# Layer 0's memory keys and values ahead of the mixer, whose input is normed before its projections

## The chip, the core and the metric

The kernel runs on one core of a Trainium2 chip. Its time is the device time of one execution in microseconds (us). The engines of the core that matter are TensorE (PE in the profile, PEld for its weight loads), VectorE (DVE), ScalarE (ACT), GpSimd (POOL) and SyncE (SP), which here only issues DMA transfers.

## The reference

The reference is a two-layer decoder trunk on one sequence of 512 tokens with 1024 channels, with 256 memory tokens beside it. All of it is float32. Cut to what the change touches:

```python
def mixer_ab(x, norm, w_in, ...):
    z = rms_norm(x, norm) @ w_in                 # 1024 -> 2560
    z_gate, z_rec, z_pool = z[..., :1024], z[..., 1024:2048], z[..., 2048:]
    xr = causal_dwconv(z_rec, conv_w, conv_b)    # 4 taps
    y_a = jax.nn.gelu(z_gate) * rg_lru(xr, ...)  # two gates, then a linear recurrence
    y_b = multi_scale_pool(z_pool, ...)          # trailing means of 2, 4, 8, 16 tokens
    return jnp.concatenate([y_a, y_b], axis=-1) @ w_out

def cross_attn(x, mem, norm, mem_norm, wq, wk, wv, wo):
    q = rms_norm(x, norm) @ wq
    m = rms_norm(mem, mem_norm)
    k, v = m @ wk, m @ wv
    ...                                          # 4 heads, softmax, then @ wo
```

Each layer is a token mixer (in layer 0 `mixer_ab`, in layer 1 a Conformer convolution), then `cross_attn`, then a gated MLP with a short convolution, each added to `x`. A last RMS norm follows. `mem` is the same in both layers; the gains and the weights are not.

## The kernel before

**Layout.** Channels lie on the 128 partitions and tokens along the free dimension, so `x` is eight tiles of 128 x 512. A weight is loaded in pieces of 128 x 1024 (512 KB). A float32 product is made of three passes of a faster format over exact parts: each operand is split into a high part (ScalarE, line 147) and a low part (VectorE or GpSimd, line 148), and `mm3` (lines 151 to 155) issues high x high, high x low and low x high. A projection of one 128-channel column chunk (`project`, line 207) is thus 24 matmuls of 512 columns; one key piece is 24 matmuls of 256 columns, and one value piece 12 of 512.

**Loads.** `load_w` (line 132) has SP load a piece into one of three "raw" buffers; then its two parts are made. Inside it the priority is rewound by 100 instructions (`AHEAD`), so a weight's load and split rank as if they had been traced 100 instructions earlier. The order of each engine's queue comes from the framework's scheduler, which takes the instructions by this priority, each when its operands and a free tile are there. Within an engine, instructions run in that order. Tiles come from pools with fixed numbers of buffers: 5 PSUM banks "mm", 2 "aux", 1 "stat"; 12 "big" tiles of 128 x 1024 in SBUF.

**Norms.** The class `Norm` (line 161) puts the gain on the operand: `feed` (line 168) makes `x * gain` on ScalarE (171) and its low part on VectorE (172), squares `x` (175) and adds up the squares (180). The token's scale `r` (a mean over channels on TensorE at 193 and 194, a square root, a reciprocal at 204) multiplies what comes out of each projection. For the first norm the additions run on GpSimd and the scale is worked out before the mixer.

**The mixer** (line 465). `recs` makes two chunks of the recurrent branch: projection, times `r` into SBUF (479), first tap on ScalarE (480), three taps on VectorE from that SBUF tile (482). `gates` makes two gate products for each chunk (494), a chain of exponentials and products, and the recurrence as a scan on VectorE (510). `gate_branch` multiplies by `r` (516) and takes GeLU (517), and `gated` multiplies both on GpSimd (521). `pool` multiplies by `r` (531) and makes window sums on GpSimd (536). The calls stand in an order written out by hand (lines 556 to 615), which mixes the three branches. The output projection (617 to 628) adds pairs of chunks to `x` at line 627.

**The memory.** `Memory` (line 217) loads `mem`, sums its squares on GpSimd (230 to 238), applies gain and token scale on VectorE (247) and splits the result. In layer 0 all this is done within the mixer, and the keys and values are projected in the attention, among its first queries (line 342, `late`). In layer 1 the keys and values are made within the MLP and the convolution of the layers before, and the attention (line 360) has only queries, scores and products.

**The start** (lines 768 to 787). SP loads a half weight piece, two tiles of `x`, the other half, more of `x`, the second piece, and the parameters. The first matmul of the mixer needs one half piece and one tile of `x`.

Of the kernel before, what the change touches and what calls it, by code (L numbers as in the profile page):

```python
# [29 lines left out]
# how the 31-tap convolution's shifts are shared out: TensorE takes them in groups of four  # L30
# [10 lines left out]
_PARAMS = [  # L41
    ("ab_norm", C), ("a_conv_w", 4 * C), ("a_conv_b", C), ("a_gate_x_b", C), ("a_gate_a_b", C),
    ("a_lambda", C), ("b_group_b", 4), ("b_scale", 4), ("c_norm", C), ("c_b_pw1", 2 * C),
    ("c_dw_w", (TAPS - 4 * min(PE_GROUPS)) * C), ("c_dw_b", C), ("c_ln_g", C), ("c_ln_b", C), ("c_b_pw2", C),
    ("xa_norm", 2 * C), ("xa_mem_norm", 2 * C), ("f_norm", 2 * C), ("f_dw_w", 6 * CF),
# [11 lines left out]
def trunk(ctx: ExitStack, tc: tile.TileContext, I: dict, out: bass.AP):  # L57
# [6 lines left out]
    big = ctx.enter_context(tc.tile_pool(name="big", bufs=12))  # L64
# [42 lines left out]
    A.dma_start(par[:, :C], I["params"][:, :C])  # L107
# [13 lines left out]
    # TensorE's clock rises only once it has been busy for a while  # L121
# [39 lines left out]
    class Norm:  # L161
        due = None

        def __init__(self, gain, late=True):
            """late: the scale is worked out behind the first projection, which doesn't need it."""
            self.gain, self.x, self.ss, self.n, self.late = gain, [None] * C, None, 0, late

        def feed(self, c, eng=None):
# [7 lines left out]
            if self.ss is None:  # L176
                self.ss = sq
            else:
                new = tmp_f()
                (eng or V).tensor_tensor(new, self.ss, sq, op=ALU.add)  # L180
                self.ss = new
            self.n += 1
            if self.n == C:
                if self.late:
                    Norm.due = self
                else:
                    self.r = rstd(self.ss)

    def mean_all(s, n=T):
        """The mean over channels of a sum over chunks, on every partition."""  # L190
# [6 lines left out]
    def rstd(s, n=T, keep=False):  # L197
        return scale_of(mean_all(s, n), n, keep)

# [17 lines left out]
    class Memory:  # L217
        r = None

        def __init__(self, layer, eng=None):  # L220
# [640 lines left out]
```

## Time and profile before

| what | us |
|---|---|
| time, median of 3 runs (1530.18 to 1530.94) | 1530.71 |
| span of the profiled execution, first to last instruction | 1528.2 |
| busy: PE, DVE, ACT, POOL | 1489.2, 951.8, 637.9, 268.2 |

The profiled execution has no time of its own in the results beside its span; the median of the runs is 2.5 us above that span. On the profile page each group of instructions has its line in the kernel, its engine, output and input tiles, shape and count, then busy time and the mean of one in ns, then the idle time of the engine just before them and what ended it. In a table of stretches each row has the stretch, its length, the busy time and count of PE, PEld, DVE, ACT and POOL, the granted TensorE clock (1.00 is full), the share of the DMA engines' time and GB/s. In a timeline a row begins with start and length, and brackets hold the idle time before it and its releaser. In the list of waits: total, times, longest.

### The profile page before, as it was taken

How to read it: one execution, taken by the hardware profiler on the slowest of the kernel's cores; microseconds unless marked ns; L12 is line 12 of the kernel's file. 1: busy time of each engine (PE TensorE's matmuls, PEld its weight loads, DVE VectorE, ACT ScalarE, POOL GpSimd, SP SyncE). 2: the span in 40 equal slices, each digit the busy share in tenths (PEclk: the TensorE clock that was granted, in tenths of full speed). 3: DMA queues.
4: the chain of work that ended last, by engine and by line, in shares of the span. 5: the costliest groups of instructions: out<-in, count | busy, mean ns of one | idle time of the engine just before them, and what ended most of it. 6: DMA issues, size and time to landing. Idle time of an engine off the chain costs nothing.

```text
span 1528.2 us, 17823 instructions
## 1 busy us (share of the span) xinstructions
PE 1489.2 (97%) x6962; PEld 1212.4 (79%) x6962; DVE 951.8 (62%) x1201; ACT 637.9 (42%) x867; POOL 268.2 (18%) x260
## 2 busy tenths in 40 slices
PE   7979999999999999999999999999999999999997
PEld 5758789888888888888887664888888888888886
DVE  8897746666655555554565996866665545555556
ACT  5766635544432323232344344644443332323223
POOL 6444100000010101010125765500001100101000
PEclk9989999999999999999999999999999999999999
DMA  5222324322222232323225543321223222222221
GB/s 192 90 87 71 111 97 145 143 97 69 97 97 97 97 111 96 111 97 110 97 83 138 166 132 103 124 97 56 70 97 97 97 96 96 97 97 96 97 83 56
DMA packets 47476, 156.23 MB, mean 102 GB/s; under 512 B 5280, under 2 KB 7328, under 8 KB 47392
## 3 DMA queue, kind: packets, MB, share of 16 engines
q1 hardware_dynamic: 46160, 154.04, 30.3%
q8 instruction: 55, 0.90, 0.2%
q10 hardware_dynamic: 1232, 1.05, 0.2%
q14 instruction: 29, 0.24, 0.0%
HBM read 144.58 MB, written 2.10 MB: 96 GB/s over the span
## 4 chain that ended last, share of the span: by engine, by line
PE 85%; DVE 8%; ACT 3%; issue 2%; POOL 2%; DMA 0%; DVEq 0%; SPq 0%; POOLq 0%; ACTq 0%
PE mm L154 27%; PE mm L155 27%; PE mm L153 27%; PE aux L678 2%; DVE big L482 1%; DVE act L172 1%; POOL tmp L536 1%; DVE wlo L148 1%; DVE act L148 1%; POOL wlo L148 1%; PE aux L155 1%; ACT whi L147 1%; POOL tmp L521 1%; PE aux L153 1%; PE aux L154 1%
## 5 line engine op out<-in xcount | busy, mean ns | idle before, releaser
L153 PE MATMUL mm<-act,whi 128*128 128x512 f32 (+1 forms) x1908 | 741.4, 389 | 12.1 <-DVE tmp L479 9.7
L154 PE MATMUL mm<-act,whi 128*128 128x512 f32 (+1 forms) x1908 | 741.8, 389 | 6.6 <-DVE act L172 3.7
L155 PE MATMUL mm<-act,wlo 128*128 128x512 f32 (+1 forms) x1908 | 740.3, 388 | 2.3 <-DVE wlo L148 2.3
L147 ACT ACTIVATE whi<-raw 128x1024 fp32r<-128x1024 f32 (+1 forms) x268 | 282.5, 1056 | 625.9 <-PE mm L154 500.7
L153 PEld LDWEIGHTS mm<-act,whi 128*128 128x128 f32 x1908 | 360.7, 189 | 87.9 <-issue 11.4
L154 PEld LDWEIGHTS mm<-act,whi 128*128 128x128 f32 x1908 | 360.9, 189 | 87.1 <-DVE act L172 7.5
L155 PEld LDWEIGHTS mm<-act,wlo 128*128 128x128 f32 x1908 | 360.8, 189 | 77.0 <-DVE wlo L148 3.4
L148 DVE TENSOR_TENSOR wlo<-raw,whi 128x1024 fp32r<-128x1024 f32 (+1 forms) x224 | 273.8, 1223 | 77.1 <-ACT whi L147 75.7
L402 POOL TENSOR_TENSOR tmp<-tmp,r 128x512 f32<-128x512 f32 x48 | 62.0, 1291 | 652.1 <-ACT tmp L401 647.2
L148 POOL TENSOR_TENSOR wlo<-raw,whi 128x1024 fp32r<-128x1024 f32 x44 | 111.6, 2541 | 126.2 <-ACT whi L147 126.1
L415 DVE TENSOR_TENSOR x<-x,mm 128x512 f32<-128x512 f32 x88 | 60.5, 687 | 99.5 <-PE mm L155 99.5
L395 DVE TENSOR_TENSOR tmp<-mm,r 128x512 f32<-128x512 f32 x48 | 33.2, 692 | 124.4 <-PE mm L155 124.4
L404 DVE TENSOR_TENSOR tmp<-mm,tmp 128x512 f32<-128x512 f32 x48 | 33.2, 691 | 95.4 <-POOL tmp L394 86.9
L696 DVE SCALAR_TENSOR_TENSOR aux<-h,par,aux 128x496 f32<-128x496 f32 (+14 forms) x105 | 75.3, 728 | 8.3 <-PE aux L678 6.0
L148 DVE TENSOR_TENSOR act<-tmp,act 128x512 fp32r<-128x512 f32 x95 | 68.6, 726 | 8.8 <-ACT act L147 8.8
L400 DVE SCALAR_TENSOR_TENSOR tmp<-tmp,par,tmp 128x512 f32<-128x512 f32 x96 | 71.9, 749 | 1.7
L401 ACT ACTIVATE tmp<-tmp 128x512 f32<-128x512 f32 x48 | 30.4, 632 | 94.9 <-DVE tmp L400 94.9
L147 ACT ACTIVATE act<-tmp 128x512 fp32r<-128x512 f32 x95 | 59.2, 625 | 23.3 <-DVE tmp L180 7.6
L394 POOL MEMSET tmp<- 128x2 f32 x48 | 4.8, 99 | 341.1 <-DVE tmp L180 341.1
L172 DVE SCALAR_TENSOR_TENSOR act<-x,par,act 128x512 fp32r<-128x512 f32 x48 | 52.2, 1095 | 8.8 <-ACT act L171 8.7
L171 ACT ACTIVATE act<-x,par 128x512 fp32r<-128x512 f32 x48 | 34.2, 712 | 13.6 <-DVE x L415 12.3
L398 ACT ACTIVATE tmp<-tmp,par 128x512 f32<-128x512 f32 x48 | 38.5, 803 | 0.8 <-DVE tmp L395 0.6
(158 smaller groups left out, 1167.0 us busy)
## 6 DMA issues: line engine op xcount, KB each, us to landing
raw<-in_wup SPq DMA_DIRECT2D x96, 512.0 KB, 3.4
raw<-in_wdown SPq DMA_DIRECT2D x48, 512.0 KB, 3.4
raw<-in_pw SPq DMA_DIRECT2D x24, 512.0 KB, 3.6
raw<-in_win SPq DMA_DIRECT2D x19, 512.0 KB, 3.6
raw<-in_wq SPq DMA_DIRECT2D x16, 512.0 KB, 3.4
raw<-in_wk SPq DMA_DIRECT2D x16, 512.0 KB, 3.4
raw<-in_wv SPq DMA_DIRECT2D x16, 512.0 KB, 4.0
raw<-in_wo SPq DMA_DIRECT2D x16, 512.0 KB, 3.4
```

The lines of the kernel that those rows point to most:

```text
L147: A.activation(hi, src, AF.Copy)
L148: (eng or V).tensor_tensor(lo, src, hi.bitcast(F32), op=ALU.subtract)
L153: PE.matmul(ps, wh, xh, start=first, stop=False)
L154: PE.matmul(ps, wh, xl, start=False, stop=False)
L155: PE.matmul(ps, wl, xh, start=False, stop=last)
L171: A.activation(hi, X[c], AF.Copy, scale=g)
L172: self.last = V.scalar_tensor_tensor(lo, X[c], g, hi.bitcast(F32), op0=ALU.mult, op1=ALU.subtract)
L398: A.activation(y, g[:, 2:], AF.Identity, scale=dw(2), bias=col("f_dw_b", layer * CF + c))
L400: V.scalar_tensor_tensor(y, g[:, j : j + T], dw(j), y, op0=ALU.mult, op1=ALU.add)
L402: G.tensor_tensor(y, y, norm.r, op=ALU.mult)
L415: V.tensor_tensor(X[n], X[n], ps, op=ALU.add)
L696: V.scalar_tensor_tensor(ps[:, s:], h[:, : T - s], tap(s, c), ps[:, s:], op0=ALU.mult, op1=ALU.add)
```

## The change

The change does four things.

- **Memory first.** The start loads `mem`, two value pieces, the parameters and then `x`. All values and keys of layer 0 are projected before the mixer. The attention of layer 0 takes the order of layer 1.
- **The memory's norm** puts only the gain on the operand (`operand`); the token scale goes to the keys as a multiplication on VectorE and to the values as a per-partition factor (`Memory.rt`). The sum of squares moves from GpSimd to ScalarE and VectorE. This holds for both layers.
- **The mixer's input** is normed in full before its projections (`Scaled`): squares on ScalarE, column sums on TensorE in the four column tiles (`quarters`, `total`), then `x * gain * r` and a split for each of eight chunks. The recurrent branch's taps, the GeLU and the pooling then read the projections from PSUM with no multiplication by `r`; the pooling copies PSUM to SBUF on ScalarE for its window sums.
- The pool of "big" tiles grows from 12 to 15, and the DMA scratch is cut to 4096 bytes.

```diff
-    A.dma_start(par[:, :C], I["params"][:, :C])
+    A.dma_start(par[:, : 3 * C], I["params"][:, : 3 * C])
...
+    class Scaled:
+        def __init__(self, gain):
+            self.gain, self.x, self.sqs, self.ps = gain, [None] * C, [], None
+        def feed(self, c):
+            sq = tmp_f()
+            A.activation(sq, X[c], AF.Square)
+            self.sqs.append(sq)
+            if c % 4 == 3:
+                if self.ps is None:
+                    self.ps = stat_ps()
+                quarters(self.ps, self.sqs)
+        def scale(self):
+            self.r = scale_of(total(self.ps, aux_ps()))
+        def split(self, c):
+            f = tmp_f()
+            V.scalar_tensor_tensor(f, X[c], col(self.gain[0], self.gain[1] + c), self.r, op0=ALU.mult, op1=ALU.mult)
+            self.x[c] = split(f)
...
+        def operand(self, h):
+            hi, lo = big_r(), big_r()
+            for j in range(4):
+                at = slice(j * M, (j + 1) * M)
+                g = col("xa_mem_norm", self.layer * C + h * 4 + j)
+                A.activation(hi[:, at], self.m[h][:, at], AF.Copy, scale=g)
+                V.scalar_tensor_tensor(
+                    lo[:, at], self.m[h][:, at], g, hi[:, at].bitcast(F32), op0=ALU.mult, op1=ALU.subtract
+                )
+            self.xs[h] = hi, lo
...
+            for h in range(2):
+                A.activation(sq[h], self.m[h], AF.Square)
+            s = sq[0]
+            V.tensor_tensor(s, s, sq[1], op=ALU.add)
+            V.tensor_tensor(s[:, : 2 * M], s[:, : 2 * M], s[:, 2 * M :], op=ALU.add)
+            V.tensor_tensor(s[:, :M], s[:, :M], s[:, M : 2 * M], op=ALU.add)
...
-            split(ps[:, :M], *blk(self.k[n // 4], (n % 4) * M, M))
+            f = tmp_f(M)
+            V.tensor_tensor(f, ps[:, :M], Memory.r, op=ALU.mult)
+            split(f, *blk(self.k[n // 4], (n % 4) * M, M))
...
-            ps = project(w or load_in("rec", c), c, norm.x)
-            z = tmp_f(T + 3)
-            G.memset(z[:, :3], 0.0)
-            V.tensor_tensor(z[:, 3:], ps, norm.r, op=ALU.mult)
-            A.activation(xr, z[:, 3:], AF.Identity, scale=col("a_conv_w", 3 * C + c), bias=col("a_conv_b", c))
-            for j in (2, 1, 0):
-                V.scalar_tensor_tensor(xr, z[:, j : j + T], col("a_conv_w", j * C + c), xr, op0=ALU.mult, op1=ALU.add)
+            ps = project(load_in("rec", c), c, norm.x)
+            A.activation(xr, ps, AF.Identity, scale=col("a_conv_w", 3 * C + c), bias=col("a_conv_b", c))
+            for s in (1, 2, 3):
+                V.scalar_tensor_tensor(
+                    xr[:, s:], ps[:, : T - s], col("a_conv_w", (3 - s) * C + c), xr[:, s:], op0=ALU.mult, op1=ALU.add
+                )
...
-            V.tensor_tensor(f, ps, norm.r, op=ALU.mult)
-            A.activation(f, f, AF.Gelu_apprx_tanh)
-            y[c] = f
+            y[c] = tmp_f()
+            A.activation(y[c], ps, AF.Gelu_apprx_tanh)
...
-            V.tensor_tensor(z[:, 16:], ps, norm.r, op=ALU.mult)
+            A.activation(z[:, 16:], ps, AF.Copy)
...
+    nc.sync.dma_start(mem.m[0][:, :T], I["mem"][0][:, :T])
+    nc.sync.dma_start(raw[0], I["wv"][0])
+    nc.sync.dma_start(mem.m[0][:, T:], I["mem"][0][:, T:])
+    nc.sync.dma_start(mem.m[1], I["mem"][1])
+    nc.sync.dma_start(raw[1], I["wv"][1])
+    nc.sync.dma_start(par[:, 3 * C :], I["params"][:, 3 * C :])
+    for c in range(C):
         nc.sync.dma_start(X[c], I["x"][c])
...
+    mem.operand(0)
+    ready = [load_w(raw=raw[0])]
+    mem.operand(1)
+    ready.append(load_w(raw=raw[1]))
+    mem.stats()
+    mem.outputs()
+    mem.values(0, ready)
     for c in range(C):
+        n0.feed(c)
+    n0.scale()
+    mem.values(1)
+    for c in range(C):
+        n0.split(c)
+    for n in range(C):
+        mem.keys(n)
```

Three lesser edits: the small chain that prepares the decay from `a_lambda` no longer waits for the norm's last operand, the columns of `xa_mem_norm` move to the front of the packed parameters, and `quarters` and `total` move out of the Conformer function.

More of the change, by code (lines that the diff above doesn't have):

```diff
@@ L198, in rstd, with quarters, total @@
         return scale_of(mean_all(s, n), n, keep)
+    def quarters(ps, xs):
+        for j in range(4):
+            n = len(xs) - 4 + j
+            PE.matmul(ps[32 * j : 32 * j + 32], onesf[:, :32], xs[n], start=n < 4, stop=n >= 4)
+    def total(ps, out):
+        f = tmp_f()
+        A.activation(f, ps, AF.Copy)
+        PE.matmul(out, fourth, f, start=True, stop=True)
+        return out
     def scale_of(ps, n=T, keep=False):
@@ L701, in conv @@
             pend.append((c, z, ps))
-        def quarters(ps, xs):
-            for j in range(4):
-                n = len(xs) - 4 + j
-                PE.matmul(ps[32 * j : 32 * j + 32], onesf[:, :32], xs[n], start=n < 4, stop=n >= 4)
-        def total(ps, out):
-            f = tmp_f()
-            A.activation(f, ps, AF.Copy)
-            PE.matmul(out, fourth, f, start=True, stop=True)
-            return out
         def merge(c, z, ps):
@@ L791, in trunk @@
     conformer(n3, n4, mem)
[L792 removed]
+    attention(1, n4, mem, n5)
     ffn(1, n5, None)
```

196 lines of the change are left out of this document (76 added, 120 removed).

## The prediction, made before the change was run

> **What bounds it now.** I read the page first, then the waits of TensorE, then a table of busy time by stretches, then the timeline.
>
> ```profile
> span 1528.2 us, 17823 instructions
> PE 1489.2 (97%) x6962; PEld 1212.4 (79%) x6962; DVE 951.8 (62%) x1201; ACT 637.9 (42%) x867; POOL 268.2 (18%) x260
> ```
> ```profile
> PE mm L153 <- DVE tmp L479: 9.7, 1, 9.7
> PE stat L194 <- DVE act L148: 5.7, 2, 5.4
> ...
> PE mm L155 <- DVE wlo L148: 2.3, 1, 2.3
> ```
> ```profile
> 0.00:29.00 29.00, 19.35 (x70) 13.14 (x70) 23.79 (x25) 16.79 (x26) 20.19 (x43) 0.97 0.65 249
> 29.00:60.00 31.00, 28.00 (x99) 22.04 (x100) 28.82 (x34) 15.33 (x20) 14.24 (x11) 0.81 0.24 74
> 60.00:116.00 56.00, 46.21 (x194) 37.23 (x193) 50.18 (x57) 43.06 (x54) 21.86 (x16) 0.91 0.24 82
> 116.00:181.60 65.60, 63.37 (x277) 51.64 (x276) 50.46 (x58) 45.40 (x60) 25.14 (x15) 1.00 0.25 82
> 181.60:780.00 598.40, 598.40 (x2846) 503.21 (x2845) 333.46 (x427) 224.75 (x304) 32.03 (x48) 1.00 0.30 105
> ...
> 1005.00:1490.00 485.00, 485.00 (x2202) 403.60 (x2201) 269.18 (x347) 175.98 (x239) 32.05 (x48) 1.00 0.27 90
> ```
> TensorE is the bound: from 181.6 to 780 us, and again from 1005 to 1490 with the second attention, its busy time equals the stretch. Its loss lies ahead of that, in the mixer, where VectorE (third busy figure) fills 102.8 of the first 116 us and is named in every long wait.
>
> ```profile
> 197.73 1.36 DVE L627 TENSOR_TENSOR x<-x,mm 128x512 f32<-128x512 f32 x2 [2.62 <-PE mm L155]
> 214.05 0.69 DVE L627 TENSOR_TENSOR x<-x,mm 128x512 f32<-128x512 f32 x1 [2.62 <-PE mm L155]
> ```
> L627 adds each finished pair of the mixer's output. Pairs come 16.32 us apart and take 72 matmuls, so a 512-column matmul issues every 0.2267 us. The first pair was done about 16.3 us before 197.7, at 181.4. Up to there the code issues 480 + 48 + 12 + 72 = 612 such matmuls (input projections, gates, pool maps, first pair), 138.7 us, and 0.7 us of norm sums. So **42 us are lost before 181.4**, and that is what the change can win.
>
> ```profile
> 5.40 0.79 PE L153 MATMUL mm<-act,whi 128*128 128x512 f32 x1
> ...
> 49.02 0.50 PE L154 MATMUL mm<-act,whi 128*128 128x512 f32 x1 [0.68 <-DVE act L148]
> ...
> 52.08 0.79 PE L155 MATMUL mm<-act,wlo 128*128 128x512 f32 x1 [2.33 <-DVE wlo L148]
> 52.67 0.63 PE L154 MATMUL mm<-act,whi 128*128 128x512 f32 x1
> ...
> 111.22 0.77 PE L153 MATMUL mm<-act,whi 128*128 128x512 f32 x1 [9.68 <-DVE tmp L479]
> 111.78 0.63 PE L154 MATMUL mm<-act,whi 128*128 128x512 f32 x1
> 112.21 0.63 PE L155 MATMUL mm<-act,wlo 128*128 128x512 f32 x1
> ...
> 115.62 0.53 PE L154 MATMUL mm<-act,whi 128*128 128x512 f32 x1
> ...
> 177.81 0.50 PE L153 MATMUL mm<-act,whi 128*128 128x512 f32 x1 [1.57 <-ACT act L147]
> ```
> Work begins at 5.4; the pauses before 29, 52 and 111 us follow, and the rest is lost in single matmuls that drip in behind the norm's operands in the first stretch. A pause costs twice: behind the 9.68 us one, matmuls issue 0.43 us apart until 115.6, some ten or eleven of them 0.2 us late, **2.2 us** more. The granted clock of the stretches (third figure from the end of each row, 0.81 and 0.91) shows the same. Behind the 1.57 us pause at 177.8 nothing of the kind follows.
>
> **The mixer after the change.** The scale multiplications go (L479, L516, L531: 20 instructions), the taps read PSUM (24), and normalising the memory leaves.
>
> ```profile
> L482 DVE SCALAR_TENSOR_TENSOR big<-tmp,par,big 128x512 f32<-128x512 f32 x24 | 28.6, 1221 | 2.1 <-ACT big L480 1.8
> L696 DVE SCALAR_TENSOR_TENSOR aux<-h,par,aux 128x496 f32<-128x496 f32 x7 | 5.1, 733 | 6.0 <-PE aux L678 6.0
> L516 DVE TENSOR_TENSOR tmp<-mm,r 128x512 f32<-128x512 f32 x8 | 5.4, 679 | 0.0
> L247 DVE SCALAR_TENSOR_TENSOR big<-big,par,r 128x256 f32<-128x256 f32 x16 | 10.3, 684 | 0.5 <-DMA big<-in_mem 0.5
> ```
> ```profile
> 104.97 5.50 DVE L482 SCALAR_TENSOR_TENSOR big<-tmp,par,big 128x512 f32<-128x512 f32 x2
> ```
> ```profile
> 10.80 8.61 DVE L172 SCALAR_TENSOR_TENSOR act<-x,par,act 128x512 fp32r<-128x512 f32 x5
> ```
> A tap from SBUF averages 1.22 us, 2.75 in the pair at 105, while GpSimd is working on weights; the conformer's taps, with a PSUM operand, take 0.73 with GpSimd equally busy. So the relief is 24 x 0.49 = 11.8, 20 x 0.68 = 13.6 and 9 for the memory (of L247's 10.3 us the half that ran here, 10.3 less 8 x 0.48, and two low parts of 1.23): VectorE falls from 129 us between 29 and 181.6 to about 95, against 138.7 of TensorE. It stops being the bound. The backlog that ended in the 9.68 us stall should go; a stall like that at 177.8 (GpSimd's product, then its split) I keep, at 3 us in all. Bounds for all that stays: 1 to 14.
>
> [...]
>
> What the taps now hold is a PSUM bank: until ScalarE's first tap and three VectorE ones are done, some 3 us, where one 0.68 us multiplication freed it; a pool group's bank waits for GpSimd's window sums too. Behind a late tap stand, in VectorE's queue, the low parts of the next weights, and TensorE waits for those. With five banks and 24 x 0.2267 = 5.4 us of matmuls to each, three free ones are 16 us of cover; without it a late bank costs its lateness and a restart, which I leave to the upper bound. That bound is the 3 us and the 10.4 of the tile rival below. ScalarE gains four pool copies and loses two splits of the memory, about even.
>
> **The opening.** 96 values matmuls and 192 key matmuls move ahead of the mixer, out of the attention.
>
> ```profile
> 246.08 0.28 PE L153 MATMUL mm<-bigr,whi 128*128 128x256 f32 x1
> 249.68 0.28 PE L153 MATMUL mm<-bigr,whi 128*128 128x256 f32 x1
> ```
> ```profile
> 941.93 1.05 PE L707 MATMUL aux<-tmp,onesf 128*32 128x512 f32 x2
> ```
> ```profile
> 3.88 0.63 ACT L147 ACTIVATE whi<-raw 128x512 fp32r<-128x512 f32 x1 [1.23 <-DMA raw<-in_win]
> 4.05 0.43 SPq L779 DMA_DIRECT2D par<-in_params  x1
> ```
> ```profile
> par<-in_params SPq DMA_DIRECT2D x1, 392.0 KB, 5.8
> ```
> Thirty key matmuls start in 3.6 us: 0.12 each. Moved work: 96 x 0.2267 + 192 x 0.12 = 44.8 us, which leaves the attention; the second layer's attention is in the new order already and keeps TensorE full (last row of the stretches), so I charge nothing there. Added: eight column sums of about 0.9 us (1.05 alone; two that share the array's columns should cost less than twice that) and a total of one such length, **8 us** (estimate, 6.4 to 9).
>
> First matmul: 256 KB were split at 3.88, and 2.44 MB had landed at 9.85 (4.05 + 5.8), 0.37 MB per us. The first 512 KB of weights then land near 5.3 and their high part is done at 6.4. But a weight load ranks as if traced 100 instructions earlier (line 133), past the loads of memory and x in SP's queue, so SP may issue the third and fourth pieces (1 MB, 2.9 us) first: 9.3. I take **8**. Behind it 5.4 MB (memory, four weight pieces, parameters, x) need some 15 us, and a piece that waits for one of three raw buffers may then queue behind x: waits of **4** (0 to 12), and **2.4** for one restart at half speed.
>
> [...]
>
> The mixer's first matmul thus comes at 8 + 44.8 + 8 + 4 + 2.4 = **67.2 us** (58 to 80). What hides the moved norm is this time; VectorE is the check:
>
> ```profile
> L148 DVE TENSOR_TENSOR wlo<-raw,whi 128x1024 fp32r<-128x1024 f32 x222 | 272.4, 1228 | 73.9 <-ACT whi L147 72.5 <-PE mm L154 0.3
> L148 DVE TENSOR_TENSOR act<-tmp,act 128x512 fp32r<-128x512 f32 x94 | 68.1, 729 | 7.5 <-ACT act L147 7.5
> L148 DVE TENSOR_TENSOR bigr<-mm,bigr 128x256 fp32r<-128x256 f32 x16 | 6.7, 417 | 0.0
> L204 DVE RECIPROCAL r<-tmp 128x512 f32<-128x512 f32 x7 | 23.5, 3351 | 12.3 <-ACT tmp L202 12.3
> ```
> 16 low parts at 1.23 = 19.6; memory operands 8 x 0.48 = 3.8 (L247 undisturbed, an estimate); memory sums and reciprocals 4.5; key outputs 8 x 0.84 = 6.7; value outputs 3; the token scale 3.35; norm and split of x 8 x (0.75 + 0.73) = 11.8; the small lambda chain 3. Sum 56, from 4.5 on: ready at 60 if never starved, below 67; ScalarE has the same pieces with shorter instructions. So the moved norm, 15 us of VectorE before its first product, lies beside the keys. If that cover goes, each us beyond 67 is one of loss.
>
> **The sum.** The first pair ends at 67.2 + 138.7 + 3 = 208.9. Before, the same work would have ended at 181.4 + 44.8 = 226.2. Gain 17.3 us. Later stages, the end and layer 1's memory (a tap more on VectorE per key piece, beside TensorE) count nothing. Span 1510.9; the median lies 2.5 above the profiled span, so **1513.4 us**.
>
> **Rivals.**
> *VectorE sets the opening's pace* (slower). If GpSimd works beside it, two-SBUF operations stretch as L172 did, 8.61 / 5 = 1.72 against 0.75. They make 37.5 of the 56 us. At 1.65 times the opening ends at 84.5 and nothing is gained: the deciding point. At 2.3 times it ends at 109, total 1555. Against: the memory's sums and the norm's additions leave GpSimd, which keeps only fills and its share of the mixer's low parts there.
> *Tiles run short.* Keys and values hold 8 of 15 "big" tiles through the mixer; the second gate group then waits for the first.
> ```profile
> 76.29 1.84 ACT L494 ACTIVATE big<-mm,par 128x512 f32<-128x512 f32 x3
> 78.92 5.36 DVE L510 TENSOR_TENSOR_SCAN big<-big,big 128x512 f32<-128x512 f32 x2
> ```
> It began at 76.3, the first ended at 84.3: 8 us, and 2.4 of slow clock: 1523.8. Against: that chain ran on a crowded VectorE.
> *A tight opening*: 58 us and 1 us of stalls, gain 28.5: 1502. For it: all low parts of the opening are undisturbed if GpSimd is idle, and TensorE's work alone is 53 us. Against: 256 KB took until 3.9 us, and 768 are needed now.
> *The backlog stays* (it doesn't do what it says): the stalls at 49 to 52 and 111 with their restarts, 3 + 2.2 + 9.7 + 2.2 = 17.1, return: 1530.5, no change. For it: sigmoids, exponentials and scans are as before. Against: the 34 us of relief fall on the engine that every wait names.
>
> **Chances.** Forecast 0.50, tight 0.18, tiles 0.17, VectorE's pace 0.09, backlog 0.06. The range 1500 to 1528 takes in forecast, tight and tiles, 0.85, with the bounds of the opening alone (58: 1504; 80: 1526). A measurement can tell 0.2%, 3 us, from no change. Faster 0.86, same 0.05, slower 0.09.
>
> **What would show it.** Right: the mixer's first input matmul at 58 to 80; no wait near 10 us behind it; taps near 0.73; the first L627-like add near 209; no new wait after it. Wrong: TensorE waiting in the opening on a weight's low part in piece after piece (VectorE or SP's order), or on a sigmoid between gate groups (tiles); or new waits in the first attention, which lost its filler.

## The result and the profile after the change

| | before | after |
|---|---|---|
| median (range), 12 runs each, us | 1530.12 (1528.94 to 1530.94) | 1529.97 (1527.66 to 1533.24) |
| ratio to before, 95% interval | | 1.0002 (0.9993 to 1.0010) |
| span of the profiled execution (its time), us | 1528.2 | 1528.0 (1529.81) |

The change makes no difference that can be measured, where 17.3 us of gain were forecast. The head of the page of the kernel after:

```profile
span 1528.0 us, 17868 instructions
PE 1496.8 (98%) x6982; PEld 1213.0 (79%) x6982; DVE 926.0 (61%) x1203; ACT 644.3 (42%) x884; POOL 241.4 (16%) x236
```

VectorE gave up 26 us of work over the whole run, and the time is the same. What TensorE waits for in the kernel after (total, times, longest):

```profile
PE mm L155 <- DVE wlo L148: 3.1, 1, 3.1
PE mm L153 <- ACT big L522: 2.7, 4, 0.9
PE mm L153 <- DVE big L508: 2.4, 1, 2.4
PE mm L153 <- ACT tmp L544: 2.2, 2, 2.0
```

The waits of 9.7 and 5.7 us of before are gone, and no wait of their length has come. In their place stand shorter ones, and half of these name ScalarE (the sigmoids, L522, and the GeLU, L544). The stretches of the kernel after, cut at the mixer's first input matmul (71.5 us) and at the first addition of the mixer's output (L650, in place of L627):

```profile
0.00:25.00 25.00, 20.83 (x77) 15.26 (x78) 15.44 (x35) 18.40 (x27) 1.65 (x28) 1.00 0.80 289
25.00:45.00 20.00, 18.97 (x64) 9.48 (x64) 12.04 (x15) 11.69 (x17) 0.00 (x0) 1.00 0.50 159
45.00:71.50 26.50, 23.38 (x195) 23.13 (x194) 24.88 (x39) 14.89 (x23) 0.11 (x1) 1.00 0.46 131
71.50:224.30 152.80, 144.57 (x612) 116.52 (x611) 101.26 (x119) 103.76 (x141) 52.18 (x31) 0.97 0.34 105
224.30:480.00 255.70, 255.70 (x1188) 213.29 (x1187) 149.23 (x205) 107.31 (x162) 10.90 (x18) 1.00 0.29 86
```
```profile
224.30 1.37 DVE L650 TENSOR_TENSOR x<-x,mm 128x512 f32<-128x512 f32 x2 [2.57 <-PE mm L155]
```

The fourth row is the mixer: 152.8 us for the 138.7 us of matmuls, so 14.1 us lost, where the prediction kept 3. TensorE is busy for 144.6 of them, so 8.2 us of the loss are pauses and some 5.9 are matmuls that ran slower. The last row shows TensorE busy through the attention and into the MLP, as assumed. The first addition comes at 224.3. Less the 44.8 us of moved work that is 179.5. Before, the first addition came at 181.6 (the prediction worked out 181.4), so 2.1 us are won in this profile. The losses ahead of the output, norm sums counted in, were 181.6 - 138.7 = 42.9 us and are 179.5 - 138.7 = **40.8**; 26.7 of it (71.5 - 44.8) now lies in the opening and 14.1 in the mixer.

TensorE in the opening of the kernel after; its timeline rows at the start and around the pauses:

```profile
6.30 1.22 PE L153 MATMUL mm<-whi,bigr 128*128 128x512 f32 x2 [0.65 <-ACT whi L147]
7.56 0.79 PE L154 MATMUL mm<-wlo,bigr 128*128 128x512 f32 x1
...
10.29 0.56 PE L155 MATMUL mm<-whi,bigr 128*128 128x512 f32 x1
10.68 0.41 PE L153 MATMUL mm<-whi,bigr 128*128 128x512 f32 x1
...
23.76 1.04 PE L224 MATMUL stat<-tmp,onesf 128*32 128x512 f32 x2 [1.14 <-ACT tmp L194]
24.74 0.73 PE L153 MATMUL mm<-whi,bigr 128*128 128x512 f32 x2
26.50 0.50 PE L154 MATMUL mm<-wlo,bigr 128*128 128x512 f32 x1 [1.03 <-DVE wlo L148]
...
39.89 1.02 PE L229 MATMUL aux<-tmp,fourth 128*128 128x512 f32 x2
...
60.11 0.39 PE L155 MATMUL mm<-bigr,wlo 128*128 128x256 f32 x1 [3.12 <-DVE wlo L148]
```

The start is earlier than forecast (6.3 instead of 8); nine matmuls take 4.4 us at half speed (0.43 from one to the next, as at 8.58, 9.01 and 9.44, against 0.23 from 10.68 on), then full speed holds to the end of the opening. One column sum, which the profile records as two matmuls, costs 0.98 (23.76 to 24.74); two of the eight ran beside each other in the same time (33.22 to 34.20). The longest wait, 3.12 us, is for a weight's low part. VectorE's rows just ahead of its end:

```profile
58.24 0.68 DVE L148 TENSOR_TENSOR act<-tmp,act 128x512 fp32r<-128x512 f32 x1
58.84 1.21 DVE L148 TENSOR_TENSOR wlo<-raw,whi 128x1024 fp32r<-128x1024 f32 x1
```

The low part stands behind the norm and the split of `x` (the first row is the last but one of these splits), which the change put there: the cover that was to hide them was used up once. The last split ended at 60.7, where the prediction had 60, well ahead of the first input matmul. The largest single loss of the mixer lies at 118 to 130 us. ScalarE's rows before it, in the kernel after:

```profile
104.78 1.25 ACT L522 ACTIVATE big<-mm,par 128x512 f32<-128x512 f32 x2
106.05 1.28 ACT L526 ACT_TABLE_LOAD   x1
107.34 1.34 ACT L526 ACTIVATE big<-big,lc 128x512 f32<-128x512 f32 x2
108.59 1.32 ACT L527 ACTIVATE big<-big,ln 128x512 f32<-128x512 f32 x2
109.81 1.14 ACT L532 ACTIVATE tmp<-big 128x512 f32<-128x512 f32 x2
...
111.92 1.28 ACT L534 ACT_TABLE_LOAD   x1
113.21 1.06 ACT L534 ACTIVATE big<-big 128x1024 f32<-128x1024 f32 x1
114.18 0.76 ACT L506 ACTIVATE big<-mm,par 128x512 f32<-128x512 f32 x1
```

VectorE's rows behind them, and the matmul that waits for the last:

```profile
110.46 1.29 DVE L533 SCALAR_TENSOR_TENSOR big<-tmp,big 128x512 f32<-128x512 f32 x2 [3.17 <-ACT tmp L532]
114.31 1.23 DVE L535 TENSOR_TENSOR big<-big,big 128x1024 f32<-128x1024 f32 x1 [2.55 <-ACT big L534]
115.45 0.74 DVE L508 SCALAR_TENSOR_TENSOR big<-mm,par,big 128x511 f32<-128x511 f32 x1
116.11 4.45 DVE L538 TENSOR_TENSOR_SCAN big<-big,big 128x512 f32<-128x512 f32 x2
120.48 2.69 DVE L508 SCALAR_TENSOR_TENSOR big<-mm,par,big 128x510 f32<-128x510 f32 x4
```
```profile
122.65 0.47 PE L153 MATMUL mm<-act,whi 128*128 128x512 f32 x1 [2.35 <-DVE big L508]
```

Read downwards: a gate block's sigmoids, exponentials, tanh, squares and square root run one after the other on ScalarE, with two table loads among them, from 104.8 to 114.2. Only then comes ScalarE's first tap of the next block (L506), and VectorE, which had been idle for 3.17 and 2.55 us in this chain, runs its scans ahead of the other taps. The taps keep their PSUM tiles until they have run, at 120 to 123, and TensorE has stood still for 2.35 us when the first of these tiles comes free at 122.65.

Another cause may play a part in this stall. GpSimd splits a weight from 115.96 to 118.36, beside the pair of scans that takes 4.45 us; the last pair ran with GpSimd idle until 204.46, and took 2.33:

```profile
202.79 2.33 DVE L538 TENSOR_TENSOR_SCAN big<-big,big 128x512 f32<-128x512 f32 x2
```

The other two pairs took 3.40 and 3.39, with GpSimd at work on 141.80 to 145.59 and 170.21 to 175.31. So some 2.1 us of the way to the taps at 120.48 go with GpSimd's work beside the scans. No run takes that work away by itself.

### The profile page after: what moved, and what is told of

The parts are those of the page before. It is cut to its first block, busy times and chain, and to the rows that moved or that the text cites. A ratio compares the mean times of both kernels' runs of the same rounds, so it can differ in the third digit from the quotient of the medians.

```text
span 1528.0 us, 17868 instructions
## 1 busy us (share of the span) xinstructions
PE 1496.8 (98%) x6982; PEld 1213.0 (79%) x6982; DVE 926.0 (61%) x1203; ACT 644.3 (42%) x884; POOL 241.4 (16%) x236
## 4 chain that ended last, share of the span: by engine, by line
PE 89%; DVE 4%; ACT 3%; POOL 1%; issue 1%; DMA 1%; SPq 0%; DVEq 0%; ACTq 0%; POOLq 0%
PE mm L153 28%; PE mm L154 28%; PE mm L155 28%; PE aux L700 2%; ACT whi L147 1%; DVE act L172 1%; PE stat L224 1%; PE aux L155 1%; PE aux L154 1%; POOL wlo L148 1%; PE aux L153 1%; PE aux L367 0%; DVE r L236 0%; DVE wlo L148 0%; DVE actf L763 0%
## 5 line engine op out<-in xcount | busy, mean ns | idle before, releaser
L147 ACT ACTIVATE whi<-raw 128x1024 fp32r<-128x1024 f32 x267 | 282.6, 1059 | 611.4 <-PE mm L154 479.0
L148 DVE TENSOR_TENSOR wlo<-raw,whi 128x1024 fp32r<-128x1024 f32 x223 | 275.7, 1238 | 69.2 <-ACT whi L147 68.5
L148 POOL TENSOR_TENSOR wlo<-raw,whi 128x1024 fp32r<-128x1024 f32 x44 | 109.0, 2480 | 159.1 <-ACT whi L147 159.1
L148 DVE TENSOR_TENSOR act<-tmp,act 128x512 fp32r<-128x512 f32 x101 | 73.7, 735 | 5.8 <-ACT act L147 5.6
L147 ACT ACTIVATE act<-tmp 128x512 fp32r<-128x512 f32 x101 | 62.9, 628 | 28.3 <-DVE tmp L180 7.6
L172 DVE SCALAR_TENSOR_TENSOR act<-x,par,act 128x512 fp32r<-128x512 f32 x40 | 35.6, 891 | 8.1 <-ACT act L171 8.0
L155 PE MATMUL mm<-bigr,wlo 128*128 128x256 f32 x128 | 36.3, 284 | 3.1 <-DVE wlo L148 3.1
```

The lines of the kernel that those rows point to most:

```text
L147: A.activation(hi, src, AF.Copy)
L148: (eng or V).tensor_tensor(lo, src, hi.bitcast(F32), op=ALU.subtract)
L155: PE.matmul(ps, wl, xh, start=False, stop=last)
L172: self.last = V.scalar_tensor_tensor(lo, X[c], g, hi.bitcast(F32), op0=ALU.mult, op1=ALU.subtract)
```

## The experiments

The measure by stage is taken from each timeline: the start of the mixer's first input matmul, the start of the first addition of its output, and the stretch between them (138.7 us of matmuls in every run). The stretch comes from one profile a run; four runs with the same mixer (after, 16 big tiles, both runs of sums) have 151.6 to 152.8. Times are medians, ratios go to the kernel before on the same chip.

| run | first input matmul | first addition | stretch | time | ratio (95%) |
|---|---|---|---|---|---|
| after | 71.5 | 224.3 | 152.8 | 1529.97 | 1.0002 (0.9993 to 1.0010) |
| 16 big tiles | 73.9 | 226.1 | 152.2 | 1529.91 | 1.0001 (0.9991 to 1.0010) |
| gates in 2 tiles | 73.9 | 233.0 | 159.1 | 1538.64 | 1.0056 (1.0041 to 1.0071) |
| taps from SBUF | 74.7 | 229.8 | 155.1 | 1533.18 | 1.0020 (1.0011 to 1.0030) |
| sums on GpSimd | 73.9 | 226.0 | 152.1 | 1529.63 | 1.0000 (0.9991 to 1.0010) |
| sums on VectorE | 71.0 | 222.6 | 151.6 | 1526.50 | 0.9976 (0.9966 to 0.9986) |
| seven PSUM tiles | 69.7 | 218.6 | 148.9 | 1589.06 | 1.0381 (1.0365 to 1.0396) |
| memory first alone | 66.6 | 224.3 | 157.7 | 1530.37 | 1.0000 (0.9990 to 1.0009) |
| mixer alone | 22.7 | 182.4 | 159.7 | 1531.00 | 1.0009 (1.0000 to 1.0018) |
| VectorE sums, gate pair split | 71.3 | 223.1 | 151.8 | 1525.02 | 0.9971 (0.9962 to 0.9981) |
| VectorE sums, squares on GpSimd | 70.4 | 222.4 | 152.0 | 1528.26 | 0.9988 (0.9978 to 0.9997) |
| VectorE sums, pool in aux | 69.5 | 220.8 | 151.3 | 1526.57 | 0.9979 (0.9969 to 0.9988) |
| VectorE sums, later tail | 71.4 | 231.6 | 160.2 | 1534.44 | 1.0018 (1.0009 to 1.0027) |
| no scan | 72.5 | 220.3 | 147.8 | 1525.68 | 0.9969 (0.9959 to 0.9978) |
| no chain | 72.8 | 217.1 | 144.3 | 1524.39 | 0.9960 (0.9945 to 0.9975) |
| neither | 73.5 | 215.1 | 141.6 | 1520.11 | 0.9927 (0.9911 to 0.9944) |

### What holds the mixer: tiles

The first theory was that the stalls are a shortage of places: PSUM tiles, held by taps, or "big" tiles, held by keys and values.

```diff
-                    ps = mm_ps()
+                    ps = aux_ps()
```

> The eight gate products' banks come from the pool of two aux banks, which the mixer leaves idle, so the projections keep all five mm banks. Theory (banks: the projections now stay in PSUM until ScalarE's and VectorE's queues reach them, and TensorE waits for a free bank): from the mixer's first input matmul to its first output addition 152.8 us shrink to 141 to 146 against 138.7 us of matmuls, the waits on the sigmoid (2.7 us), on the taps (2.4) and the 1.0 on the pooling copy go, the time falls by 7 to 11 us to 1519 to 1523. Rival (big tiles run short: a gate group waits for the tiles of the one before): the stretch stays within 2 us of 152.8, the time within 2 us of 1530. Rival (ScalarE's load itself): the sigmoid waits go but come back on the splits or the GeLU, less than 4 us gained.

It is 0.56% slower. The waits of that run between 70 and 235 us:

```profile
PE mm L153 <- DVE tmp L567: 6.5, 1, 6.5
PE aux L153 <- ACT big L522: 4.6, 2, 4.0
```

Two tiles are too few for four gate products, and the wait on them (second row) has taken the place of the others. This says nothing against more tiles.

```diff
-    act = ctx.enter_context(tc.tile_pool(name="act", bufs=32))
-    big = ctx.enter_context(tc.tile_pool(name="big", bufs=15))
+    act = ctx.enter_context(tc.tile_pool(name="act", bufs=31))
+    big = ctx.enter_context(tc.tile_pool(name="big", bufs=16))
```

> One more big tile (16 for 15, one act tile less to make room). Rival of big tiles: a gate group starts earlier, the mixer's stretch shrinks by 4 us or more. Theory of banks: no change, within 2 us of 1530, mixer's stretch 152.8 within 1 us.

Nothing changes, so the "big" tiles don't bind. The order of instructions is that of the kernel after: the run also shows that the opening scatters, 73.9 here against 71.5, with the same work. Its first addition, less the moved work, is at 181.3, so the 2.1 us that the profile of after had won there lie within this scatter.

```diff
-    psum = ctx.enter_context(tc.tile_pool(name="ps", bufs=5, space=bass.MemoryType.PSUM))
+    psum = ctx.enter_context(tc.tile_pool(name="ps", bufs=7, space=bass.MemoryType.PSUM))
-    aux = ctx.enter_context(tc.tile_pool(name="aux", bufs=2, space=bass.MemoryType.PSUM))
...
     def aux_ps():
-        return aux.tile([P, T], F32, tag="aux", name=nm("aux"))
+        return psum.tile([P, T], F32, tag="mm", name=nm("aux"))
```

> The five mm and two aux banks become one pool of seven, so that projections, pool groups and gate products of the mixer share seven banks and none is reserved; the work is the same. Theory (banks): the mixer's stretch, from its first input matmul to its first output addition, 152.2 to 152.8 us with five banks, falls to 142 to 147, the waits on sigmoid, taps and pooling copy go, the time falls to 1520 to 1525. The run with the gate products on two banks of their own (stretch 159) is then explained by its two banks being too few. Rival (the chain through ScalarE and VectorE from one gate group to the next is late by itself): the stretch stays at 150 to 155 and the waits move to other instructions.

The time is worthless here, for it is 59 us longer: TensorE's longest total of waits, 39.4 us, lies in the Conformer, which used the two tiles by themselves. In the mixer the sigmoid waits are gone, a tap wait of 2.0 us stays, and the stretch falls to 148.9, by 3.3 to 3.9 us. Two more tiles are worth about a quarter of the loss; what still more would give, no run shows.

### What the parts are worth

Taps from SBUF again, with VectorE's copy in place of the old multiplication:

```diff
-            A.activation(xr, ps, AF.Identity, scale=col("a_conv_w", 3 * C + c), bias=col("a_conv_b", c))
-            for s in (1, 2, 3):
...
+            z = tmp_f(T + 3)
+            G.memset(z[:, :3], 0.0)
+            V.tensor_copy(z[:, 3:], ps)
+            A.activation(xr, z[:, 3:], AF.Identity, scale=col("a_conv_w", 3 * C + c), bias=col("a_conv_b", c))
+            for j in (2, 1, 0):
...
```

> The recurrent branch alone goes back to SBUF: VectorE copies each projection out of PSUM (8 copies of about 0.5 to 0.7 us) and ScalarE's and VectorE's taps read that copy, as in the kernel before but with no multiplication by the token scale. Theory of banks: a bank is held for one copy, the wait of 2.4 us on the taps goes, the mixer's stretch shrinks by 3 to 7 us although the taps slow down beside GpSimd (from 0.73 to about 1.2 us, 24 of them, 11 us of VectorE). Rival (VectorE's load decides, PSUM reading is a gain by itself): the stretch grows by 5 to 12 us and the time with it, to 1535 to 1542.

It is 0.2% slower, some 3 us, and 2.3 to 2.9 of them lie in the mixer's stretch. The taps of the kernel after, between 71.5 and 224.3:

```profile
L508 DVE SCALAR_TENSOR_TENSOR big<-mm,par,big 128x511 f32<-128x511 f32 (+2 forms) x24 | 17.6, 744 | 4.9 <-ACT big L506 4.5
```

and of this run, between 70 and 235:

```profile
L511 DVE SCALAR_TENSOR_TENSOR big<-tmp,par,big 128x512 f32<-128x512 f32 x24 | 22.6, 941 | 6.8 <-ACT big L509 6.3
```

Reading PSUM pays: 744 ns against 941, and the copy saved (685 ns, 8 times). The medians of one tap are alike, 748 and 752 ns; the difference is in single taps, of which none takes more than 750 from PSUM and some take up to 2211 from SBUF. The tap wait went, as the theory of tiles expected, but the sigmoid waits grew from 2.7 to 8.0 us.

The memory first, with the mixer's norm, multiplications by `r` and taps as before:

```diff
-    n0 = Scaled(("ab_norm", 0))
+    n0 = Norm(("ab_norm", 0))
...
-    n0.scale()
+    Norm.due = None
+    n0.r = rstd(n0.ss)
...
+            z = tmp_f(T + 3)
+            G.memset(z[:, :3], 0.0)
+            V.tensor_tensor(z[:, 3:], ps, norm.r, op=ALU.mult)
...
+            V.tensor_tensor(y[c], ps, norm.r, op=ALU.mult)
...
+            V.tensor_tensor(z[:, 16:], ps, norm.r, op=ALU.mult)
```

> Memory first as in the change, but the mixer keeps the old norm: the gain on the operand, the token scale multiplied on VectorE as each projection leaves PSUM, taps from SBUF. This undoes the half of the change that reads PSUM. The prediction's theory (VectorE's load was what stalled the mixer): the stretch of the mixer grows from 152 to 158 to 170 us, the time to 1535 to 1548. Rival (early release of a bank by one VectorE instruction is worth as much as the relief of VectorE): the stretch stays at 148 to 155, and with no split of normed x and no column sums the opening is 3 to 8 us shorter: 1520 to 1528.

And the mixer's part with the memory in the attention, as before:

```diff
-    mem.values(0, ready)
     for c in range(C):
         n0.feed(c)
     n0.scale()
-    mem.values(1)
     for c in range(C):
         n0.split(c)
-    for n in range(C):
-        mem.keys(n)
...
-    mixer(n0, n1)
-    attention(0, n1, mem, n2)
+    mem = Memory(0)
+    mixer(n0, n1, mem)
+    attention(0, n1, mem, n2, True)
```

> The other half alone: the norm ahead of the projections and the reading from PSUM as in the change, but the memory's operands, keys and values where the kernel before has them, after the mixer and in the attention; x is loaded first. The norm then has no matmuls to lie beside. If the mixer's own order is what makes its stretch 152 us, it is 150 to 155 here too; if the memory's tiles and late work beside it are the cause, it is 141 to 147. The first input matmul comes at 24 to 30 us (x lands by 10, squares, sums, scale, first split), so the time is 1523 to 1532 in the first case and 1512 to 1522 in the second.

Neither part moves the time, alone or together. By stages they do: the memory alone has its first input matmul at 66.6, and a stretch of 157.7. Adding the mixer's part takes VectorE's work in the stretch from 120.5 us to 101.3, shortens the stretch by 4.9 to 5.5 us and delays the first matmul by 4.9 to 7.3. That is the cancellation inside the change. The longest wait of the memory-first run between 60 and 230 us, and that of the mixer's part alone up to 190, are for operands of TensorE that ScalarE makes:

```profile
PE mm L153 <- ACT act L147: 8.1, 2, 6.9
```
```profile
PE mm L153 <- ACT act L147: 6.7, 1, 6.7
```

With the first, a long wait like that of the kernel before is back (6.9 us in one piece, there 9.68). The second ends at 22.7, with the mixer's first input matmul: it is the norm of `x` with nothing beside it, and no part of that run's stretch. The stretch of 159.7 fits neither of the two cases that were expected for it; a wait of 4.2 us for a weight's low part lies in it.

### The opening: who adds the squares

In place of `quarters` and `total`, GpSimd or VectorE adds the squares of `x` (the two runs differ in the one letter):

```diff
-            if c % 4 == 3:
-                if self.ps is None:
-                    self.ps = stat_ps()
-                quarters(self.ps, self.sqs)
+            if self.ps is None:
+                self.ps = sq
+            else:
+                new = tmp_f()
+                V.tensor_tensor(new, self.ps, sq, op=ALU.add)
+                self.ps = new
...
-            self.r = scale_of(total(self.ps, aux_ps()))
+            self.r = rstd(self.ps)
```

> The squares of x are added up on GpSimd, as in the kernel before, and meaned with two matmuls, in place of eight column sums and a total on TensorE. Theory (the column sums cost TensorE about 8 us in line in the opening): the mixer's first input matmul comes at 63 to 66 us for 71.5, the time falls by 5 to 8. Rival (the opening is paced by the weights' arrival or by VectorE, the sums fill pauses): it stays within 2 us of 71.5, or comes later since VectorE's two-operand instructions slow down beside GpSimd.

> The squares of x are added on VectorE (7 additions of 0.68 us), then meaned with two matmuls; no column sums on TensorE. With GpSimd's additions TensorE waited 3.5 us for their chain and restarted at half speed. Theory (the column sums' 8 to 9 us of TensorE are a real cost in the opening): the mixer's first input matmul at 65 to 69 us for 71.5 to 73.9, the time 1523 to 1527. Rival (the weights' arrival paces the opening, and the sums only keep TensorE running in its pauses): 71 to 74, with pauses and half-speed restarts where the sums were, and the time within 2 us of 1530.

On GpSimd nothing is won: TensorE is rid of the sums' 8 us and waits for them (3.5 us on L214), and it has two half-speed spells (26.5 to 31.4 and 42.3 to 45.3). On VectorE 0.24% is won, 0.14 to 0.34, though a new wait of 5.4 us comes for a key's PSUM tile and the waits for a weight's high part grow from 0.6 to 3.4. The time is what the theory expected, but the first input matmul, at 71.0, is where the rival had it: the waits took most of what the sums had cost. That run's longest waits between 40 and 230 us:

```profile
PE mm L153 <- DVE tmp L304: 5.4, 1, 5.4
PE mm L153 <- ACT big L523: 2.7, 4, 0.9
PE mm L153 <- DVE big L509: 2.4, 1, 2.4
```

The first row is new, the other two are those of the kernel after, unmoved. So the mixer's loss doesn't come from the opening.

### What holds the mixer: one wait moved after another

Three variants of the run with VectorE's sums, each with one edit:

```diff
-                    ps = mm_ps()
+                    ps = mm_ps() if g is ga else aux_ps()
```

> Whole-row sums on VectorE as in the run with no column sums, and of each pair of gate products the second takes a PSUM tile of the two auxiliary ones, the first one of the five. If banks held behind ScalarE's sigmoids and taps are what the mixer's stalls are made of, the four sigmoid waits (2.7 us) and the tap wait (2.4 us) near 118 us go, with about half of the half-speed spell behind them: the stretch from the first input matmul to the first output addition falls from 151.6 to 145 to 148 us, and the time from 1526.5 to about 1521. If the waits only move from one bank to another, as they did with both gate products in the two tiles, the stretch stays at 150 to 154 and the time at 1525 to 1530.

```diff
-                A.activation(sq, a[:, at], AF.Square)
+                G.tensor_tensor(sq, a[:, at], a[:, at], op=ALU.mult)
```

> Whole-row sums on VectorE, and the squares of the gates' decay (16 of about 0.7 us) on GpSimd in place of ScalarE. If ScalarE's chain of a gate block sets the taps' delay, ScalarE's first taps come about 1.4 us earlier per block and the tap wait near 118 us (2.4 us) shrinks below 1.2: the time is 1523 to 1526. If the block's own chain (exp, tanh, square, sqrt, scan, one after the other) sets it, GpSimd's slower squares make it longer: the tap and scan waits grow by 1 to 3 us each block and the time is 1528 to 1535.

```diff
-            ps = project(load_in("pool", g), g, norm.x)
+            ps = project(load_in("pool", g), g, norm.x, aux_ps())
```

> Whole-row sums on VectorE, and the four pooled groups' projections take an auxiliary PSUM tile in place of one of the five, which they hold through ScalarE's copy, GpSimd's window sums and VectorE's three finishing operations (some 8 us each). If the held bank is what the taps and sigmoids run short of, the waits at 118 to 126 us (2.4 and 0.9 to 2.7 us) go and the time is about 1521 to 1524, with the first output addition 3 to 5 us earlier than 222.6. If not, the waits stay where they are and the time at 1525 to 1528.

The stretch stays at 151.3 to 152.0 in all three: the waits change their names, not their sum. In the first, the sigmoids' rows are gone and a pool's operand and a GeLU have grown (2.7 and 3.2 us). Its time is the best of the kernels that do all the work, 1525.0, but its interval overlaps that of 1526.5. In the second, the sigmoid waits have grown to 4.5 us (it moves 8 squares of 0.62 us, not the 16 of 0.7 that were expected). Then the order: the second half of a gate block behind the next projections.

```diff
             V.tensor_tensor(gx, gx, xr, op=ALU.mult)
+            return b, ga, gx, a
+
+        def tail(b, ga, gx, a):
...
-        gates(*r0)
+        t0 = gates(*r0)
         r2 = recs(2)
+        tail(*t0)
```

> Whole-row sums on VectorE as in the run with no column sums; beside that each gate block is cut in two where its sigmoids end, and its second part (exponential, tanh, squares, square root, scan) is written behind the next projections instead of ahead of them; the instructions are the same but for a table load. If what is left of the mixer's stalls is the gate block's chain on ScalarE and VectorE standing ahead of the next taps in their program order, the tap wait near 119 us (2.4 us) and the waits behind it go, ScalarE's first taps come at once behind their projections, and the stretch from the first input matmul to the first output addition falls from 151.6 to 143 to 147 us, the time from 1526.5 to 1518 to 1523. If the stalls follow from the number of PSUM tiles or from the sum of the engines' work, they come back at the sigmoids or GeLUs: stretch 150 to 154, time 1525 to 1530.

It is slower, and the stretch 160.2. ScalarE's first tap comes 5 us sooner, as meant, and VectorE's queue then carries the same chain among the taps; TensorE's waits come back at the sigmoids, 7.9 us in all. VectorE's rows:

```profile
115.53 0.75 DVE L509 SCALAR_TENSOR_TENSOR big<-mm,par,big 128x511 f32<-128x511 f32 x1 [2.15 <-ACT big L507]
116.20 1.66 DVE L537 SCALAR_TENSOR_TENSOR big<-tmp,big 128x512 f32<-128x512 f32 x1
117.79 0.73 DVE L509 SCALAR_TENSOR_TENSOR big<-mm,par,big 128x510 f32<-128x510 f32 x1
```

This order doesn't settle it, so the work itself was left out, of the kernel after. First the scans:

```diff
-                V.tensor_tensor_scan(gx[:, at], a[:, at], gx[:, at], 0.0, op0=ALU.mult, op1=ALU.add)
```

> The changed kernel with the eight scans of the recurrence left out (the gated input stands in for the hidden state), so VectorE loses 13.6 us of its 101 in the mixer and TensorE, ScalarE and GpSimd nothing. If the remaining stalls are VectorE's work standing ahead of the taps, the tap wait (2.4 us) and the pool's wait behind it near 120 us go: the stretch from the first input matmul to the first output addition falls from 152.2 to 143 to 147 us and the time from 1529.9 to 1519 to 1524. If it is ScalarE's chain, the sigmoid and GeLU waits stay: stretch 149 to 152, time 1526 to 1530.

Then ScalarE's operations of the block (28 with the four square roots, not 24):

```diff
-                A.activation(a[:, at], ga[:, at], AF.Exp, scale=lc[:, c : c + 1])
-                A.activation(ga[:, at], ga[:, at], AF.Tanh, scale=ln[:, c : c + 1])
...
-                sq = tmp_f()
-                A.activation(sq, a[:, at], AF.Square)
-                V.scalar_tensor_tensor(ga[:, at], sq, 1.0, ga[:, at], op0=ALU.add, op1=ALU.mult)
-            A.activation(ga, ga, AF.Sqrt)
+                V.scalar_tensor_tensor(a[:, at], gx[:, at], 1.0, ga[:, at], op0=ALU.add, op1=ALU.mult)
```

> The changed kernel with the gate block's exponential, tanh, squares and square root left out (24 operations and 8 table loads of ScalarE, 29.9 us of its 104 in the mixer; VectorE keeps as many operations as before, on sigmoid values). If the remaining stalls are ScalarE's chain ahead of the first taps and the sigmoids, they go: stretch 142 to 146, time 1518 to 1524. If it is VectorE's taps and scans, the tap wait stays and the stretch is 149 to 152, the time 1526 to 1530.

With both edits in one kernel:

> Both left out, the scans and ScalarE's chain of the gates. If the stalls are the two engines' latency one behind the other, only this run brings the stretch to the 138.7 us of matmuls and some 3 (141 to 143), and the time to 1516 to 1520. If stalls of over 8 us stay (stretch above 147), neither engine's gate work makes them, and the PSUM tiles or the weights' arrival do.

The mixer's stretch in the three runs, one row of the stretches from each:

```profile
72.50:220.30 147.80, 141.69 (x613) 115.14 (x612) 83.40 (x109) 102.63 (x138) 48.24 (x31) 0.99 0.33 105
```
```profile
72.80:217.10 144.30, 139.81 (x613) 114.17 (x612) 99.36 (x118) 72.78 (x101) 56.48 (x31) 1.00 0.34 107
```
```profile
73.50:215.10 141.60, 139.25 (x613) 114.31 (x612) 85.24 (x110) 73.18 (x101) 53.06 (x31) 1.00 0.35 110
```

Against 152.5 (the mean of 152.8 and 152.2), no scans win 4.7 us, no ScalarE chain 8.2, neither 10.9. With neither the stretch is 141.6, 2.9 above the matmuls, and one kind of wait is left in it:

```profile
PE mm L153 <- ACT big L522: 2.3, 3, 0.9
```

The second row is the telling one. VectorE is busy for 99.4 us, nearly as long as with this work in place (101.3), yet 8.2 of the 14 us are gone: VectorE's sum of work does not by itself make the stalls. The gate block's work on both engines makes all but 2.9 us of them, of which ScalarE has the larger part and the scans (with their stretching beside GpSimd) the other. Whether it does so as a chain, by its length, or as time that it fills in two queues, these runs do not separate: ScalarE's own work falls from 103.8 to 72.8 us in the second row, and VectorE's to 83.4 in the first. The rows at 104.8 to 122.65 speak for the chain, since VectorE is idle twice in it. For the run without scans 143 to 147 or 149 to 152 was expected, and it fell between the two; the times of the other two, 1524.4 and 1520.1, lie just above what was expected for them.

## Why the prediction was wrong, point by point

**The bound** was read rightly: TensorE, with 42 us lost ahead of the mixer's first output pair. That these 42 us "is what the change can win" holds as a bound; 2.1 of them were won in one profile and 0.3 in that of the same order with 16 tiles.

**VectorE's relief** came about: taps at 744 ns where 733 were taken, 101.3 us of work in the mixer where about 95 were, and the 9.68 us wait is gone. A copy of PSUM to SBUF ahead of a ScalarE tap and three VectorE taps did not pay: the run with it was 0.20% slower than the kernel before (0.11 to 0.30), which the kernel after equals.

**The step that failed** is the next one: "The backlog that ended in the 9.68 us stall should go; a stall like that at 177.8 (GpSimd's product, then its split) I keep, at 3 us in all." 13.5 to 14.1 us stayed, at the upper bound that was written for them (14). The step took VectorE's sum of work for the cause of the stalls. With that sum 37 us below TensorE's, stalls remained: in the largest, a gate block runs across two engines, and VectorE stands idle for part of the time while the taps behind it wait. The last three runs show that this block's work holds the rest of the loss: with it left out the stretch is 141.6 us, what the prediction had (138.7 + 3 = 141.7). The queue behind a late tap was named in the prediction, with the right consequence ("a late bank costs its lateness and a restart"), but it was put into the bound and not into the sum.

**The opening** came at 71.5 to 73.9 instead of 67.2, inside 58 to 80. Its terms for 71.5: first matmul 6.3 for 8; moved work 44.8, unchanged; sums 7 x 0.98 (two of the eight at once) + 1.02 = 7.9 for 8; restart 4.4 - 9 x 0.2267 = 2.3 for 2.4; the rest, waits, 10.2 for 4 (0 to 12). That last term is the mis-sized one: 3.12 us of it is the weight's low part behind the norm of `x`, the others to be seen are pauses of 0.5 to 1.1 us, and together they come to 6.6. What the other 3.6 us are stays open; the 44.8 was not measured by itself. The first matmul was early because the memory and the first two pieces did go first in SP's queue, from 0.74 to 3.05. The third and fourth pieces passed only the parameters and `x`, whose loads began at 7.9 and 8.4.

**The sum**: in the profile of after 4.3 us from the opening and 11.1 from the mixer take 15.4 off the forecast gain of 17.3, and in that with 16 tiles 6.7 and 10.5 take 17.2. Behind the first addition nothing was to change, and the spans agree to 0.2 us, though the profile of after entered the MLP 2.2 us earlier (its first addition at 478.2, before at 480.4) and lost it again later; the run with 16 tiles entered it at 480.1.

**The rivals**: the big tiles are refuted by the run with 16; the waits on a sigmoid, which were to be their sign, did come, and went with two more PSUM tiles. VectorE's pace did not set the opening in the way that was feared (GpSimd did 0.11 us between 45 and 71.5, and the split of `x` ran at 0.68), though VectorE was busy for 24.9 of those 26.5 us and the longest wait is for it. The rival "the backlog stays" gave the right time, 1530.5, by luck: the stalls that it named did go, and others came.

## What to carry to other kernels

An engine that is named in every long wait can be the last link of a chain and not only the one that is short of time (here 19 us less work on it shortened the stretch by 5): before pricing its relief, look whether it stands idle between those waits, and follow one block's operations across the engines from its PSUM tile to the release of that tile. A cheap test before a rebuild is to leave out the suspected work and to read the stretch, as the last three runs did. And a norm that is moved ahead of its products paid here at the front what it saved behind; a gain, 0.24%, came only with VectorE's sums.

## What the runs showed of the hardware

In one execution, the spells of half-speed matmuls (0.43 us from one to the next, against 0.23) end near whole multiples of 3.41 us apart (the nine below to within 0.3 us). TensorE's rows in the kernel after, at the ends of two such spells, one stretch of the timeline each:

```profile
129.44 0.63 PE L153 MATMUL mm<-act,whi 128*128 128x512 f32 x1
129.87 0.50 PE L154 MATMUL mm<-act,whi 128*128 128x512 f32 x1
```
```profile
211.24 0.63 PE L155 MATMUL mm<-act,wlo 128*128 128x512 f32 x1
211.67 0.56 PE L153 MATMUL mm<-act,whi 128*128 128x512 f32 x1
```

From 129.87 to 211.67 are 81.8 us, 24 times 3.41, and from the end in the opening (10.29) to 129.87 are 119.6, 35 times 3.42. Other traces show the same length: before, spells end at 33.80, 57.79 and 115.62, 7 times 3.43 and 24 times 3.41 behind the first, and in the run with the later tail at 127.37, 161.29 and 219.58, 10 times 3.39 and 27 times 3.42 behind the first. Of all lengths from 2 to 5 us, 3.41 fits these nine ends best. So the same pause can cost more or fewer slow matmuls by where it falls (an estimate from these ends), which may be one reason why runs with equal instructions scatter. The spell that ended at 129.87 followed pauses of 2.35 us and less.
